# A hybrid decoder layer on one core: two factor broadcasts placed later among the first projections, and the last row statistics placed half a gate earlier

## The chip, the core and the metric

The kernel runs on one core of a Trainium2 chip. A core has a matrix engine (TensorE, PE in the profile), a vector engine (VectorE, DVE), an activation engine (ScalarE, ACT), GpSimd (POOL) and a queue engine that issues transfers (SyncE, SP). The metric is the device time of one execution in microseconds (us). Before the change it is 1122.99 us (median of 3 runs, 1122.89 to 1123.69). A difference of about 0.2%, some 2.2 us, is what a measurement of this kernel can tell from none.

## What is computed

One decoder layer on 512 tokens of width 1024, all in float32. A retention branch and a latent attention branch read the same normalised input through one combined projection; their gated sum goes through an output projection into the residual; then a squared-ReLU MLP, then a gated per-layer embedding. The parts that the change touches are these:

```python
h = rms_norm(x, norm_mix)
proj = h @ w_in
rq, rk, rv, rg, cq, ckv, krope, gr, gm = split(proj)
cq, ckv = rms_norm(cq, q_lat_norm), rms_norm(ckv, kv_lat_norm)
q = cq @ w_uq                       # 8 heads of 128 + 64
kv = ckv @ w_ukv                    # 8 heads of 128 (keys) + 128 (values)
k = concat(k_nope, krope)           # the 64 rotary columns are shared by the heads
q, k = rms_norm(q, q_norm), rms_norm(k, k_norm)     # then rotated by position
mixed = sigmoid(gr) * a_ret + sigmoid(gm) * a_mla
...
gate = sigmoid(rms_norm(x, norm_ple) @ w_ple_gate)
return x + gate * (p_l @ w_ple)
```

## The kernel before

Tokens lie along the free axis (512 columns) and channels along the 128 partitions, so a projection is a row of 128x512 matmuls into one bank of PSUM. Every float32 operand is split into a high and a low half (`split`, L301: ScalarE writes the high half, VectorE the low half), and a product is three matmuls, low by high, high by low, high by high (`mm3`, L291). Weights come as chunks: a transfer into a raw buffer (`wr_`, L243, six buffers), a copy on ScalarE (`wh_`, L261) and a subtraction on VectorE (`wl_`, L265), three buffers each. A chunk's split is queued one chunk ahead of its use (`AHEAD`), its transfer three ahead (`PREP`).

The work is a list of steps written by hand (`step`, L207; the list is L1119 to L1310). `run_steps` records them in that order, and the matmuls stay in it. The order of the other engines' instructions is set by a scheduler when the program is built, from the order of recording and what each needs. A step with a key uses a chunk of weights; a step without one uses none. PSUM has eight banks in the first part, each held until its last reader is done.

Row normalisation is postponed: the input enters its projections with its gain but unnormalised (`xg`), and sums of squares give factors that are multiplied in later. `first_stats` (L431) turns the first sums around with four transposes (`fst`) and computes on VectorE, in small instructions of a few columns, first `rx` (the input's inverse root mean square, by three Newton rounds, `rsqrt`, L322), then `rl` (the same for the two latents, again three rounds), from them `rho`, and `f` (the buffers `f1` and `f2`, by which values and statistics are scaled). A factor holds one number for each token, on partitions; to multiply a tile that has tokens along its columns, it is broadcast by four transposes on TensorE (`bcast`, L342). Two such broadcasts are touched here: `x_factor` (L459) writes `prx` from `rx`, which ScalarE copies into `rbc`, and `rotary_key` (L507) writes `prho` from `rho`, after which VectorE rotates the shared key columns (`t`, `krot`) and the split gives `kph` and `kpl`, which the attention scores (`sc`) read.

Around them stand `kq_head` (keys and queries of one head, `pk` and `pq`), `value_pair` (values of two heads, `pv`, 24 matmuls of 256 columns, scaled by `f` on their way out), `query_rotary` (`pqa`, `pqb`, 18 matmuls), `rotary_out` (rotates the query columns on VectorE, `o` and `qt`, and sends sixteen copies `qp` by SP's queue), `gate_out` (L685, multiplies a finished gate `gm` by `rbc` into `zm`, which goes to memory), and `fill` (L1112), which takes the next half gate from a list of fillers: 12 matmuls of the gate `gm` that nothing nearby waits for. `rotary_stats` (`sqr`), `pair_sums` (`sums`), `pair_stats` (`st`, then `ha`, `hr`) and `head_factor` (`pbk`) lead on to the first scores.

At the end, `turn` transposes the MLP's result back and adds the residual, `token_stats` (L955) sums squares into `stx` and computes `rx3`, `token_factor` (L962) broadcasts that into the same PSUM tile and ScalarE copies it out as `bcx`. `ple_gate` (L1088) computes gate `n` (`pg`, 24 matmuls, in two halves of 12 where `part` is given), and `ple_out` (L1097) multiplies it by `bcx`, takes the sigmoid (`zg`), multiplies by `pw`, adds and stores. This part has four PSUM tiles of two banks each.

Of the kernel before, what the change touches and what calls it, by code (L numbers as in the profile page):

```python
# [147 lines left out]
def trunk_layer(ctx: ExitStack, tc: tile.TileContext, xT, pT, pos, gains, const, decay, wstream, outT):  # L148
# [58 lines left out]
    def step(key, fn, *args):  # L207
        steps.append((key, fn, args))
# [903 lines left out]
    def fill(n=1):  # L1112
        for _ in range(n):
            if fillers and fillers[0][0] is None:
                step(*fillers.pop(0))
            if fillers:
                step(*fillers.pop(0))
# [11 lines left out]
    step(("kq", 0), kq_head, 0)  # L1129
    step(None, first_stats)  # L1130
    step(("kq", 1), kq_head, 1)
    step(None, x_factor)
    step(None, gate_out, 0)
    step(None, rotary_key)
    step(("v", 0), value_pair, 0)
    step(("qr", 0), query_rotary, 0)
    step(None, mask_parts)
    step(None, rotary_out, 0)
    fill(3)
    step(None, rotary_stats, 0)  # L1140
    step(None, pair_sums, 0)
    fill(1)
# [153 lines left out]
    step(("ple", 1), ple, 3)  # L1296
    step(None, turn, 2)
    step(None, turn, 3)
    for part in range(2):
        for n in range(2):  # L1300
            step(("pg", n), ple_gate, n, part)
    step(None, token_stats, "x3", "sq3")
    step(("pg", 2), ple_gate, 2)
    step(None, token_factor, "x3")
    step(None, ple_out, 0)
    step(None, ple_out, 1)
    step(None, ple_out, 2)
# [47 lines left out]
```

## Time and profile before

| what | number |
|---|---|
| time, median of 3 runs | 1122.99 us |
| the profiled execution's own time | 1123.06 us |
| its span, first to last instruction | 1121.3 us |
| TensorE busy | 1102.3 us |
| VectorE, ScalarE, GpSimd busy | 735.2, 537.2, 85.6 us |
| mean transfer rate over the span | 157 GB/s |

The span leaves out 1.76 us of the execution's own time. A row of the waits says which engine and line waited, for whom, the total in us, how often, and the longest. A row of the timeline has the start, the duration, engine, line, operation, tiles and shapes; in square brackets stands the idle time ahead of it and what ended it. A matmul's duration is longer than its distance to the next, since neighbours overlap; distances are taken from starts.

### The profile page before, as it was taken

What the parts mean: (1) busy time and instruction counts of PE and PEld (TensorE: products, weight loads), DVE (VectorE), ACT (ScalarE), POOL (GpSimd) and SP (SyncE); (2) the same over time, 40 slices, a digit from 0 to 9 for tenths busy, and PEclk for the clock granted to TensorE, in tenths of its full rate; (3) what the DMA queues carried; (4) which work ended last, traced back from release to release, by engine and by line L of the source; (5) the groups of instructions that cost most, each with busy time, mean ns of one, the idle gap of its engine ahead of it and who ended that gap; (6) DMA issues with size and microseconds to landing.
All of it is one profiled execution on the core that took longest, in us unless ns stands there. A gap on an engine that the chain in (4) does not pass through costs nothing.

```text
span 1121.3 us, 14666 instructions
## 1 busy us (share of the span) xinstructions
PE 1102.3 (98%) x5529; PEld 933.9 (83%) x5529; DVE 735.2 (66%) x1195; ACT 537.2 (48%) x763; POOL 85.6 (8%) x113
## 2 busy tenths in 40 slices
PE   9979999999999999999999999999999999999998
PEld 6767888888889889888988987888888888888877
DVE  7677676656776845855683677555465666668675
ACT  7635656453365435355544544434443444445542
POOL 0000000000110020021003000010100100101000
PEclk9989999999999999999999999999999999999999
DMA  7224131356787274589639754693755755738401
GB/s 256 70 70 133 53 104 61 126 180 216 197 220 185 98 201 130 151 176 256 161 105 216 218 179 158 190 283 107 179 160 163 184 164 153 184 122 227 139 29 76
DMA packets 59223, 175.97 MB, mean 157 GB/s; under 512 B 7248, under 2 KB 8656, under 8 KB 58896
## 3 DMA queue, kind: packets, MB, share of 16 engines
q1 hardware_dynamic: 45168, 129.66, 34.1%
q0 software_dynamic: 13840, 45.36, 20.9%
q8 instruction: 43, 0.70, 0.2%
q14 instruction: 28, 0.23, 0.1%
q10 hardware_dynamic: 144, 0.03, 0.0%
HBM read 156.92 MB, written 15.99 MB: 154 GB/s over the span
## 4 chain that ended last, share of the span: by engine, by line
PE 92%; DVE 3%; ACT 2%; issue 1%; DMA 1%; SPq 0%; DVEq 0%; ACTq 0%
PE up L168 16%; PE dn L168 14%; PE rg L168 7%; PE rv L168 7%; PE br L168 6%; PE pg L168 4%; PE gr L168 4%; PE rq L168 4%; PE bm L168 4%; PE rk L168 4%; PE gm L168 4%; PE wo L168 4%; PE ro L168 3%; PE sc L168 2%; PE pcq L168 1%; PE rs L168 1%
## 5 line engine op out<-in xcount | busy, mean ns | idle before, releaser
L168 PE MATMUL dn<-wh_dn,cl 128*128 128x512 f32 x224 | 87.2, 389 | 0.0
L168 PE MATMUL dn<-wh_dn,ch 128*128 128x512 f32 x224 | 87.2, 389 | 0.0
L168 PE MATMUL dn<-wl_dn,ch 128*128 128x512 f32 x224 | 87.1, 389 | 0.0
L261 ACT ACTIVATE wh_dn<-wr_dn 128x1024 fp32r<-128x1024 f32 x32 | 34.0, 1062 | 75.5 <-PE up L168 54.3
L261 ACT ACTIVATE wh_up<-wr_up 128x1024 fp32r<-128x1024 f32 x32 | 34.0, 1061 | 58.0 <-PE up L168 29.3
L265 DVE TENSOR_TENSOR wl_dn<-wr_dn,wh_dn 128x1024 fp32r<-128x1024 f32 x32 | 39.1, 1220 | 27.5 <-ACT wh_dn L261 27.5
L265 DVE TENSOR_TENSOR wl_up<-wr_up,wh_up 128x1024 fp32r<-128x1024 f32 x32 | 39.1, 1222 | 18.2 <-ACT wh_up L261 18.1
L265 DVE TENSOR_TENSOR wl_rg<-wr_rg,wh_rg 128x1024 fp32r<-128x1024 f32 x20 | 24.5, 1224 | 38.7 <-ACT wh_rg L261 38.3
L168 PEld LDWEIGHTS dn<-wh_dn,cl 128*128 128x128 f32 x224 | 42.1, 188 | 8.8
L168 PEld LDWEIGHTS dn<-wh_dn,ch 128*128 128x128 f32 x224 | 42.1, 188 | 8.8
L980 DVE SCALAR_TENSOR_TENSOR f<-up,bcx 128x512 f32<-128x512 f32 x32 | 20.6, 686 | 43.8 <-PE up L168 43.8
L168 PEld LDWEIGHTS dn<-wl_dn,ch 128*128 128x128 f32 x224 | 42.1, 188 | 8.6
L261 ACT ACTIVATE wh_dn<-dr_dn 128x1024 fp32r<-128x1024 f32 x24 | 25.5, 1060 | 41.6 <-PE up L168 28.8
L223 POOL DMA_DIRECT2D dr_dn<-wstream x24 | 21.7, 906 | 305.4 <-DMA dr_dn<-wstream 181.9
L265 DVE TENSOR_TENSOR wl_dn<-dr_dn,wh_dn 128x1024 fp32r<-128x1024 f32 x24 | 29.3, 1222 | 22.1 <-ACT wh_dn L261 22.1
L261 ACT ACTIVATE wh_rv<-wr_rv 128x1024 fp32r<-128x1024 f32 x28 | 29.7, 1060 | 28.1 <-PE rv L168 11.5
L261 ACT ACTIVATE wh_rg<-wr_rg 128x1024 fp32r<-128x1024 f32 x28 | 29.5, 1055 | 25.8 <-DMA wr_rg<-wstream 20.5
L265 DVE TENSOR_TENSOR wl_br<-wr_br,wh_br 128x1024 fp32r<-128x1024 f32 x16 | 19.5, 1221 | 21.6 <-ACT wh_br L261 21.6
L1038 DVE TENSOR_TENSOR d<-d,dn 128x1024 f32<-128x1024 f32 x24 | 29.3, 1219 | 6.5 <-PE dn L168 6.5
L265 DVE TENSOR_TENSOR wl_rv<-wr_rv,wh_rv 128x1024 fp32r<-128x1024 f32 x20 | 24.4, 1224 | 12.2 <-ACT wh_rv L261 12.2
L869 ACT ACTIVATE rt<-br 128x512 f32<-128x512 f32 x24 | 14.3, 597 | 36.1 <-PE br L168 30.7
L223 POOL DMA_DIRECT2D wr_rg<-wstream x16 | 13.9, 870 | 161.2 <-DVE wl_br L265 93.1
(1813 smaller groups left out, 3620.5 us busy)
## 6 DMA issues: line engine op xcount, KB each, us to landing
wr_up<-wstream SPq DMA_DIRECT2D x32, 512.0 KB, 4.4
wr_dn<-wstream SPq DMA_DIRECT2D x32, 512.0 KB, 3.5
dr_dn<-wstream POOLq DMA_DIRECT2D x24, 512.0 KB, 7.4
wr_rv<-wstream SPq DMA_DIRECT2D x20, 512.0 KB, 4.1
wr_rg<-wstream SPq DMA_DIRECT2D x20, 512.0 KB, 4.5
wr_rv<-wstream POOLq DMA_DIRECT2D x16, 512.0 KB, 6.0
wr_rg<-wstream POOLq DMA_DIRECT2D x16, 512.0 KB, 7.5
wr_br<-wstream SPq DMA_DIRECT2D x16, 512.0 KB, 3.5
```

The source lines that it names most:

```text
L168: return tc.keep_in_program_order(nc.tensor.matmul(*a, **k))
L223: nc.gpsimd.dma_start(raw, chunk(("w", blk, kb, fb, c)), accum_op=ALU.add)
L261: i = ACT(hi, raw, AF.Copy, scale=sign)
L265: TT(lo, raw, hi.bitcast(F32), op=ALU.subtract)
L869: ACT(t, ps, AF.Copy)
L980: STT(u[:, i], ps[:, i], 0.0, V["bcx2"], op0=ALU.max, op1=ALU.mult)
L1038: TT(to, to, dps[p], op=ALU.add if sign > 0 else ALU.subtract)
```

## The change

Two places of the step list are reordered; no instruction is added or taken away.

```diff
     step(("kq", 1), kq_head, 1)
+    step(("v", 0), value_pair, 0)
     step(None, x_factor)
     step(None, gate_out, 0)
-    step(None, rotary_key)
-    step(("v", 0), value_pair, 0)
     step(("qr", 0), query_rotary, 0)
     step(None, mask_parts)
     step(None, rotary_out, 0)
-    fill(3)
+    fill(1)
+    step(None, rotary_key)
+    fill(2)
     step(None, rotary_stats, 0)
...
     step(None, turn, 3)
-    for part in range(2):
-        for n in range(2):
-            step(("pg", n), ple_gate, n, part)
+    for n in range(2):
+        step(("pg", n), ple_gate, n, 0)
+    step(("pg", 0), ple_gate, 0, 1)
     step(None, token_stats, "x3", "sq3")
-    step(("pg", 2), ple_gate, 2)
+    step(("pg", 1), ple_gate, 1, 1)
+    step(("pg", 2), ple_gate, 2, 0)
     step(None, token_factor, "x3")
+    step(("pg", 2), ple_gate, 2, 1)
     step(None, ple_out, 0)
```

In the first place the values of the first pair go ahead of the broadcast of `rx`, and the broadcast of `rho` with the rotation of the key goes behind the rotary queries and one half gate. Keyed steps keep their order, so chunks are fetched in the same order as before.

TensorE's order after the second head's queries `pq`, before the change (each row is one matmul, output<-inputs and its shape, x4 four alike):

```order
L168 MATMUL pq_602<-cq2l,wh_kq_494 128x512
L168 MATMUL pq_602<-cq2h,wh_kq_494 128x512
L168 MATMUL prx<-cst,rx 128x128 x4
L168 MATMUL prho<-cst,rho 128x128 x4
L168 MATMUL pv_652<-wh_v_585,ckv0l 128x256
L168 MATMUL pv_652<-wl_v_586,ckv0h 128x256
```

The same place of TensorE's order after the change, with the middles of the groups `pv`, `pqa`, `pqb` and `gm` left out:

```order
L168 MATMUL pq_602<-cq2h,wh_kq_494 128x512
L168 MATMUL pv_624<-wh_v_585,ckv0l 128x256
...
L168 MATMUL pv_643<-wh_v_585,ckv1h 128x256
L168 MATMUL prx<-cst,rx 128x128 x4
L168 MATMUL pqa_679<-cq0h,wl_qr_621 128x512
...
L168 MATMUL gm_750<-xg3h,wh_gm_0_675 128x512
L168 MATMUL prho<-cst,rho 128x128 x4
L168 MATMUL gm_750<-xg4h,wl_gm_1_747 128x512
```

24 matmuls of `pv` now stand ahead of `prx`, and these with 18 of `pqa` and `pqb` and 12 of `gm` ahead of `prho`. Behind that half gate comes its second half, and then the next gate's first half (`gm_808`), which reads the weight half `wl_gm_0_783`.

On VectorE, in the difference where `rl` is computed, rows with a minus stood there before and rows with a plus stand there now (`al` is what `rl` is the inverse root of, `nt` a scratch tile, `ad` and `skr` parts of the key's statistics):

```order
-L687 TENSOR_TENSOR zm_625<-gm_454,rbc 128x512
+L577 COPY ad_826<-skr 128x4 x2
 L325 TENSOR_SCALAR rl<-al 128x8
-L510 TENSOR_TENSOR t_634<-kz,tmc 64x512
+L577 COPY ad_830<-skr 128x4 x2
 L326 TENSOR_SCALAR rl<-rl 128x8
-L511 SCALAR_TENSOR_TENSOR t_635<-kz,cst,tms 64x512
+L577 COPY ad_1721<-skr 128x4 x2
 L328 TENSOR_TENSOR nt_556<-rl 128x8
```

The wide `zm` and the two wide products `t`, and a third `t` a few rows below, have left the chain of `rl`; one wide `wl_gm_1_747` has come into it.

VectorE's order behind the first low halves of the values, after the change, down to the weight half that the second gate needs:

```order
L687 TENSOR_TENSOR zm_669<-gm_454,rbc 128x512
L312 SCALAR_TENSOR_TENSOR v00l<-pv_624,f_570,v00h 128x256
L312 SCALAR_TENSOR_TENSOR v01l<-pv_643,f_570,v01h 128x256
L555 SCALAR_TENSOR_TENSOR o_705<-pqa_679,gn,tmc 128x512
L556 SCALAR_TENSOR_TENSOR qt_708<-pqa_679,gn,tms 128x512
L557 SCALAR_TENSOR_TENSOR qt_707<-pqb_689,gn,tms 128x512
L558 SCALAR_TENSOR_TENSOR o_706<-pqb_689,gn,tmc 128x512
L559 TENSOR_TENSOR o_705<-o_705,qt_707 128x512
L560 TENSOR_TENSOR o_706<-o_706,qt_708 128x512
L561 TENSOR_TENSOR sa_701<-sa_701,sb_702 128x512
L307 TENSOR_TENSOR qr10l<-o_705,qr10h 128x512
L265 TENSOR_TENSOR wl_gm_0_783<-wr_gm_0_780,wh_gm_0_782 128x512
```

The rotation of the key, which stood ahead of the values' low halves, has moved behind this piece, between and behind the weight halves of the following gates; `zm` has moved into it.

At the end, TensorE's order after the change around the sums of squares `stx` (the first gates are `pg_9442` and `pg_9461`, the third `pg_9524`, the fourth `pg_9579`):

```order
L168 MATMUL pg_9442<-x3g7h,wh_pg_9357 128x512
L168 MATMUL stx_9486<-ones,sq_9434 128x1 x4
L168 MATMUL pg_9461<-x3g4h,wl_pg_9437 128x512
...
L168 MATMUL pg_9524<-x3g3h,wh_pg_9455 128x512
L168 MATMUL stx_9486<-cst,rx_9492 128x128 x4
L168 MATMUL pg_9524<-x3g4h,wl_pg_9456 128x512
...
L168 MATMUL pg_9579<-x3g0h,wl_pg_9519 128x512
```

Before, the sums stood behind the last matmul of `pg_9461`, 12 matmuls later, and the broadcast behind the last of the third gate, straight ahead of the fourth. The distance between the two stays at 24 matmuls.

## The prediction

> **What bounds the kernel now.** I read the page first, then TensorE's waits, then the granted clock by stretch, then the timelines around the longest waits. The page's first two parts and its chain:
>
> ```profile
> span 1121.3 us, 14666 instructions
> PE 1102.3 (98%) x5529; PEld 933.9 (83%) x5529; DVE 735.2 (66%) x1195; ACT 537.2 (48%) x763; POOL 85.6 (8%) x113
> PE 92%; DVE 3%; ACT 2%; issue 1%; DMA 1%; SPq 0%; DVEq 0%; ACTq 0%
> ```
>
> TensorE is the bound, busy for 98% of the span and 92% of the chain. A reordering can gain only where TensorE stands still or runs slowly: some 19 us in all. Its waits, longest first:
>
> ```profile
> PE prho L168 <- DVE rl L451: 6.1, 1, 6.1
> PE pg L168 <- ACT bcx L965: 1.2, 1, 1.2
> PE prx L168 <- DVE rx L330: 1.1, 1, 1.1
> PE pbk L168 <- DVE hr L603: 1.0, 1, 1.0
> ```
>
> The first three are the waits at the moved steps. The windows view (length, busy time and instructions of the five engines, granted clock, DMA) shows a second loss behind them:
>
> ```profile
> 54.50:62.50 8.00, 0.82 (x6) 0.46 (x5) 7.53 (x42) 2.98 (x7) 0.72 (x1) 0.79 0.30 104
> 63.20:67.40 4.20, 4.20 (x27) 4.20 (x26) 2.54 (x4) 1.33 (x3) 0.00 (x0) 0.67 0.00 0
> 112.40:115.40 3.00, 3.00 (x28) 2.93 (x25) 0.82 (x4) 2.76 (x8) 0.00 (x0) 1.00 0.00 0
> 1089.00:1095.00 6.00, 6.00 (x26) 4.96 (x27) 4.40 (x7) 1.38 (x3) 0.00 (x0) 1.00 0.21 83
> ```
>
> In the first window TensorE is busy for 0.82 of 8 us, while VectorE works for 7.53: it computes the factors. In the second, the values of the first pair run at a granted clock of 0.67 and take 4.2 us; the same 24 matmuls of the next pair take 3.0 at 1.00 (third window). So an idle of 6.1 us drops the clock. One of 1.2 us does not: the fourth window, behind the wait for `bcx`, shows 1.00.
>
> **The change, step by step.** The places on TensorE's timeline, in the order of before:
>
> ```profile
> 54.27 0.39 PE L168 MATMUL pq<-cq2h,wh_kq 128*128 128x512 f32 x1
> 55.77 0.65 PE L168 MATMUL prx<-cst,rx 128*128 128x128 f32 x4 [1.12 <-DVE rx L330]
> 62.48 1.09 PE L168 MATMUL prho<-cst,rho 128*128 128x128 f32 x4 [6.06 <-DVE rl L451]
> 77.03 0.50 PE L168 MATMUL gm<-xg0h,wl_gm 128*128 128x512 f32 x1
> 40.70 5.44 PE gm L168 x24
> 84.80 0.44 PE st L168 x4
> ```
>
> The two last rows are of the chain: 24 matmuls of 512 columns take 5.44 us, 0.227 each; four transposes with the restart behind them 0.44. The row at 77.03 is the first matmul of the second gate `gm`, from where TensorE's order is as before. The question of the first place is when that matmul starts.
>
> TensorE alone: `pv` follows `pq` at 54.27 + 0.23 = 54.5 and takes 3.0 at full clock, to 57.5. `prx` finds `rx` done (55.7) and takes 0.44. The 18 matmuls of the rotary queries take 4.1, to 62.0, the half gate 12 x 0.227 = 2.7, to 64.7, `prho` 0.44, the second half 2.7: **67.9**. By TensorE alone the gain is 77.0 - 67.9 = 9.1: the waits of 7.2, the slow clock's 1.2 in `pv`, and 0.7 of slow or delayed broadcasts.
>
> VectorE holds the weight half `wl_gm` of that matmul, behind the values and the whole rotation of the queries. Its rows before:
>
> ```profile
> 57.53 0.69 DVE L687 TENSOR_TENSOR zm<-gm,rbc 128x512 f32<-128x512 f32 x1
> 58.21 0.68 DVE L510 TENSOR_TENSOR t<-kz,tmc 64x512 f32<-64x512 f32 x1
> 59.00 0.75 DVE L511 SCALAR_TENSOR_TENSOR t<-kz,cst,tms 64x512 f32<-64x512 f32 x1
> 59.93 0.68 DVE L512 TENSOR_TENSOR t<-t,t 64x512 f32<-64x512 f32 x1
> 62.45 0.17 DVE L454 TENSOR_SCALAR f<-rl 128x4 f32<-128x4 f32 x1
> 67.68 0.48 DVE L312 SCALAR_TENSOR_TENSOR v00l<-pv,f,v00h 128x256 fp32r<-128x256 f32 x1 [0.54 <-ACT v00h L309]
> 68.09 0.48 DVE L312 SCALAR_TENSOR_TENSOR v01l<-pv,f,v01h 128x256 fp32r<-128x256 f32 x1
> 70.32 0.75 DVE L555 SCALAR_TENSOR_TENSOR o<-pqa,gn,tmc 128x512 f32<-128x512 f32 x1 [0.62 <-ACT sa L552]
> 70.98 0.74 DVE L556 SCALAR_TENSOR_TENSOR qt<-pqa,gn,tms 128x512 f32<-128x512 f32 x1
> 73.75 0.68 DVE L559 TENSOR_TENSOR o<-o,qt 128x512 f32<-128x512 f32 x1
> 74.34 0.69 DVE L560 TENSOR_TENSOR o<-o,qt 128x512 f32<-128x512 f32 x1
> ```
>
> By the distances of starts a wide two-input instruction costs 0.60, a three-input one 0.66, one of 256 columns 0.4. Four wide ones leave the chain of `rl` (3 x 0.60 + 0.66 = 2.5) and one `wl_gm` enters (0.6). The removed ones also filled gaps in which the chain waited for itself; I leave 0.2 for that. So `f` comes 1.7 sooner, at 60.8. ScalarE's first value copy and its hand-over take some 0.8 (an estimate: one half of this size, 0.48 in the rows of VectorE, and the two hand-overs), so the first `v00l` starts at 61.6. From there to the end of `wl_gm` stand four value halves (1.6), `zm` (0.6), four three-input products (2.6), three sums (1.8), `qr10l` (0.6) and `wl_gm` itself (0.7): 7.9 us, to 69.5. The rotary key, which goes behind this, isn't in it. The second gate starts at **69.6**, and a wait of 1.7 is new. Gain of the first place: 77.0 - 69.6 = **7.4 us**. The bounds of the new wait, which no row shows: nothing, if ScalarE and VectorE overlap better (gain 9.1), and twice as much (gain 5.7); I take the middle, which is the sum of the rows.
>
> Does it last? The rotary key's three products, two `krot` and `kpl`, 3.7 us on VectorE, ran while TensorE stood still or in `pv`. They now go between 69.6 and the first head's statistics, where VectorE waited before:
>
> ```profile
> 80.89 0.24 DVE L578 TENSOR_TENSOR ad<-sqr,f 128x8 f32<-128x8 f32 x2 [1.52 <-PE sqr L168]
> 84.84 0.69 DVE L687 TENSOR_TENSOR zm<-gm,rbc 128x512 f32<-128x512 f32 x1 [3.11 <-PE gm L168]
> 89.07 0.17 DVE L603 TENSOR_TENSOR hr<-hr,f 128x16 f32<-128x16 f32 x1
> 90.57 1.03 PE L168 MATMUL pbk<-cst,hr 128*128 128x128 f32 x8
> 90.77 0.69 DVE L687 TENSOR_TENSOR zm<-gm,rbc 128x512 f32<-128x512 f32 x1 [0.70 <-PE gm L168]
> 75.68 1.23 SPq L567 DMA_DIRECT2D qp<-qr10h  x2
> 85.70 0.58 SPq L567 DMA_DIRECT2D qp<-qr20l  x1
> ```
>
> 1.52 + 3.11 of idle time take 3.7 with 0.9 to spare. `hr` is done 1.3 us ahead of its broadcast; the new order puts a weight half of 640 columns in front of its last steps (0.75, by the 0.60 of 512), and 0.6 remains. The sixteen copies `qp` on SP's queue move with `qr10h`, some 7 us sooner, and the first scores, which need four of them, come behind `pbk`, 15 us after the first issue. Without that cover each microsecond of lateness is one of TensorE's. From 90.77 to 109 the chain runs over VectorE and ScalarE (the angles, the exponentials), but its start waits 0.70 for TensorE's gate, so it moves along. Here I count nothing. `gate_out` keeps the first gate's bank 4 to 5 us longer; the eight banks just suffice, since values and `zm` are read before 69.6. SP's and POOL's queues keep their orders.
>
> The last place:
>
> ```profile
> 1077.35 0.68 DVE L1084 TENSOR_TENSOR sq<-sq 128x512 f32<-128x512 f32 x1
> 1078.06 0.40 PE L168 MATMUL pg<-x3g4h,wl_pg 128*128 128x512 f32 x1
> 1084.98 0.16 DVE L330 SCALAR_TENSOR_TENSOR rx<-nt,rx 128x4 f32<-128x4 f32 x1
> 1087.19 0.60 PE L168 MATMUL stx<-cst,rx 128*128 128x128 f32 x4
> 1088.98 0.50 PE L168 MATMUL pg<-x3g0h,wl_pg 128*128 128x512 f32 x1 [1.19 <-ACT bcx L965]
> ```
>
> The fourth gate starts 1.79 behind the broadcast, because it takes over the PSUM tile that ScalarE is still copying out; without the wait it would be 0.44, so 1.35 are to be had. The broadcast now ends half a gate, 2.7 us, ahead of the fourth gate, which covers that. The sums of squares move to 1078.06, and `sq` is done at 1078.03: a tie, for which I take off 0.05. `rx3` keeps its slack of 2 us before the broadcast. Gain: **1.3 us**, bounds 0.9 (`sq` late by half a microsecond) and 1.4.
>
> **Sum:** 7.4 + 1.3 = 8.7. The profiled execution took 1123.06, so **1114.36**; the median lies 0.07 below it: **1114.3 us**.
>
> [...] The clock was kept at an idle of 1.2 us and lost at one of 6.1; the new wait of 1.7 is near the first, so the sum has no slow clock in it. [...] The rows here leave open where between 1.2 and 6.1 it falls.
>
> **The rivals.**
> 1. *VectorE's backlog returns part of it.* If the 3.7 us of the key don't fit, `pbk` waits. At worst all but the slack of 1.3 shows: 2.4, so 1116.7. Against it: the idle time sums to 4.6.
> 2. *The clock falls at the new wait*: 1.2 more, 1115.5. Against it: the fourth window.
> 3. *The first gain is hidden anyway.* If the VectorE and ScalarE chain from 90 to 109 did not move with TensorE, the scores would come when they came before, and only the end would gain: 1121.7. Against it: that chain's start waits for TensorE.
> 4. *Slower: the query copies come late.* The sixteen copies stand on SP's queue behind two weight loads that wait for buffers. If these held the copies, the first scores would wait for `qp`. They are needed just behind `pbk`, at about 84; each microsecond beyond that is one of the total, so from a landing at 84 + 8.7 = 92.7 the kernel is slower than before, and with copies at 95 it takes 1125. Against it: the buffers are freed sooner than before, and even the last copy, issued at 85.7 before, would be issued at 78.7, 14 us ahead of that point.
>
> **How the numbers follow.** Forecast 0.76; rival 1 0.09, rival 2 0.07, rival 3 0.05, rival 4 0.03. The forecast and the first two rivals are faster by more than 0.2% (2.2 us, about what a measurement can tell from no change): 0.92. Rival 3 is within it, 0.05; rival 4 slower, 0.03. The range goes down to 1112.3 (no new wait: 1.7, and some more) and up to 1117.0, which takes in the doubled wait with an end that gains 0.9 (1116.5) and the first two rivals.
>
> **What would show it.** In TensorE's waits the rows of `prho`, `prx` and `pg` on `bcx` are gone, and one of `gm` on `wl_gm`, 1.7, is new. `pv` shows a clock of 1.00 and 3.0 us. The second gate starts at 69.6, `pbk` near 83.2, the fourth gate of the end 8.7 sooner with no wait. I am wrong if `pbk` or the scores show a new wait, if the clock drops behind 68, or if the first matmul of the second gate starts behind 71.

## The result and the profile after

| kernel | median (runs) | ratio to before, 95% interval |
|---|---|---|
| before | 1122.94 us (1122.50 to 1123.69, 4 runs) | 1 |
| changed | 1114.07 us (1113.85 to 1117.37, 4 runs) | 0.9929 [0.9912, 0.9946] |

The change takes off 8.87 us; 8.7 were forecast. One of the four runs took 1117.37, the other three lie within 0.4 of each other.

The page of the changed kernel, its span, its engines and the chain that ended last:

```profile
span 1112.4 us, 14663 instructions
PE 1100.3 (99%) x5529; PEld 932.8 (84%) x5529; DVE 734.8 (66%) x1195; ACT 536.9 (48%) x763; POOL 85.8 (8%) x113
PE 92%; DVE 4%; ACT 1%; DMA 1%; issue 1%; SPq 0%; DVEq 0%; ACTq 0%
```

The span is 8.9 shorter, but TensorE's busy time only 2.0: most of what went was standing still, and the 2.0 are mostly matmuls that had run at a slow clock (1.3 of them in `pv`, 4.2 us before and 2.87 now). Its waits, the longest but for one of 1.5 at the start that both kernels have:

```profile
PE gm L168 <- DVE wl_gm L265: 1.5, 1, 1.5
...
PE pbk L168 <- DVE hr L603: 1.0, 1, 1.0
PE sc L168 <- ACT sqk L526: 0.8, 1, 0.8
PE pt0a L168 <- DVE p L652: 0.7, 1, 0.7
```

The rows of `prho` (6.1), `prx` (1.1) and `pg` on `bcx` (1.2) are gone, and one of `gm` on `wl_gm` is new. The row of `pbk` is no news: it belongs to a later pair of heads (at 161 us, before at 169) and stood there before with the same 1.0. The windows view of the first place, first over the window that held TensorE's long idle before, then over the values, then over the new wait (columns as in the prediction, granted clock third from the end):

```profile
54.50:62.50 8.00, 8.00 (x49) 7.05 (x48) 7.46 (x47) 4.71 (x12) 0.00 (x0) 1.00 0.30 93
53.80:56.80 3.00, 3.00 (x27) 2.96 (x26) 2.79 (x15) 2.60 (x6) 0.00 (x0) 1.00 0.29 87
67.40:70.00 2.60, 1.05 (x6) 0.90 (x6) 2.60 (x5) 1.15 (x2) 0.00 (x0) 1.00 0.25 64
```

VectorE works as hard in the first window as before (7.46 to 7.53), but TensorE is now busy for all of its 8 us instead of 0.82. The clock stays at 1.00, also through the new wait. TensorE's timeline at the points that the prediction named:

```profile
53.67 0.39 PE L168 MATMUL pq<-cq2h,wh_kq 128*128 128x512 f32 x1
53.89 0.28 PE L168 MATMUL pv<-wh_v,ckv0l 128*128 128x256 f32 x1
56.76 0.60 PE L168 MATMUL prx<-cst,rx 128*128 128x128 f32 x4
64.06 0.60 PE L168 MATMUL prho<-cst,rho 128*128 128x128 f32 x4
68.95 0.47 PE L168 MATMUL gm<-xg0h,wl_gm 128*128 128x512 f32 x1 [1.54 <-DVE wl_gm L265]
```

From the last `pq` to the second gate it is 68.95 - 53.67 = 15.28 us; before it was 77.03 - 54.27 = 22.76. The place gained **7.48**. Distances must be taken here: executions reach this stage up to 0.8 us apart (the marks `fst` in the table below), which lies ahead of the change. VectorE's rows on the path of that wait:

```profile
59.98 0.17 DVE L454 TENSOR_SCALAR f<-rl 128x4 f32<-128x4 f32 x1
60.84 0.48 DVE L312 SCALAR_TENSOR_TENSOR v00l<-pv,f,v00h 128x256 fp32r<-128x256 f32 x1 [0.19 <-ACT v00h L309]
68.12 0.69 DVE L265 TENSOR_TENSOR wl_gm<-wr_gm,wh_gm 128x512 fp32r<-128x512 f32 x1
81.97 0.17 DVE L603 TENSOR_TENSOR hr<-hr,f 128x16 f32<-128x16 f32 x1
```

From the start of `v00l` to the end of `wl_gm` VectorE works 7.97 us without a gap, and TensorE waits for that end. `hr` ends at 82.14. The end of the kernel:

```profile
1060.42 1.91 PE L168 MATMUL tr<-cst,d 128*128 128x128 f32 x16
1069.86 0.68 DVE L1084 TENSOR_TENSOR sq<-sq 128x512 f32<-128x512 f32 x1
1070.68 1.02 PE L168 MATMUL stx<-ones,sq 128*128 128x1 f32 x8
1077.77 0.60 ACT L965 ACTIVATE bcx<-stx 128x512 f32<-128x512 f32 x1 [2.09 <-PE stx L168]
1080.33 0.39 PE L168 MATMUL pg<-x3g0h,wl_pg 128*128 128x512 f32 x1
```

`sq` ends at 1070.54, just ahead of its sums at 1070.68; `bcx` is copied 2 us ahead of the fourth gate, which starts with no wait.

### The profile page after: what moved, and what is told of

Same layout as the page of the kernel before. It is cut to its first block, busy times and chain, and to the rows that moved or that the text cites. A ratio compares the mean times of both kernels' runs of the same rounds, so it can differ in the third digit from the quotient of the medians.

```text
span 1112.4 us, 14663 instructions
## 1 busy us (share of the span) xinstructions
PE 1100.3 (99%) x5529; PEld 932.8 (84%) x5529; DVE 734.8 (66%) x1195; ACT 536.9 (48%) x763; POOL 85.8 (8%) x113
## 4 chain that ended last, share of the span: by engine, by line
PE 92%; DVE 4%; ACT 1%; DMA 1%; issue 1%; SPq 0%; DVEq 0%; ACTq 0%
PE up L168 16%; PE dn L168 14%; PE rg L168 7%; PE rv L168 7%; PE br L168 6%; PE pg L168 4%; PE gr L168 4%; PE rq L168 4%; PE bm L168 4%; PE rk L168 4%; PE wo L168 4%; PE gm L168 3%; PE ro L168 3%; PE sc L168 2%; PE pcq L168 1%; PE rs L168 1%
```

## The experiments

All times were taken beside the kernel before on the same chip. The changed kernel itself ran beside experiments 4 to 6; 1, 2, 3 and 7 ran on another chip. To see the first place by itself I also take, from each trace, the distance from the transposes of the first statistics (`fst`, which stand ahead of both moved steps) to the first head's broadcast `pbk` (which stands behind everything that was moved there):

| kernel | median us (runs) | ratio to before | `fst` | `pbk` | distance |
|---|---|---|---|---|---|
| before | 1122.94 (the 4 above) | 1 | 50.61 | 90.57 | 39.96 |
| changed, beside the runs | 1113.93 (1113.85 to 1114.66) | 0.9920 [0.9907, 0.9932] | 50.12 | 82.58 | 32.46 |
| first place alone | 1115.06 (1114.80 to 1115.61) | 0.9929 [0.9917, 0.9942] | 50.12 | 82.53 | 32.41 |
| last place alone | 1121.26 (1120.60 to 1122.44) | 0.9985 [0.9976, 0.9994] | 49.92 | 90.78 | 40.86 |
| key back, values moved | 1119.16 (1117.56 to 1120.16) | 0.9963 [0.9950, 0.9975] | 49.86 | 87.80 | 37.94 |
| values back, key moved | 1114.24 (1113.79 to 1115.72) | 0.9920 [0.9906, 0.9933] | 50.32 | 83.21 | 32.89 |
| key's products doubled | 1117.59 (1115.45 to 1119.60) | 0.9947 [0.9934, 0.9961] | 50.68 | 85.19 | 34.51 |
| queries' rotation later | 1119.73 (1118.66 to 1120.27) | 0.9968 [0.9957, 0.9980] | 50.09 | 88.55 | 38.46 |
| sums into the new wait | 1112.54 (1112.14 to 1112.85) | 0.9906 [0.9893, 0.9920] | 50.20 | 81.58 | 31.38 |

**1. The first place alone.** The end's part of the diff undone.

> The first place alone; the end as before. Theory (the two places gain apart from each other, 7.4 to 7.5 us in the first and 1.2 to 1.3 in the last): 1115.4 us, the second gate's first matmul at 69.0 with a wait of 1.5 on wl_gm, and the wait of pg on bcx back at 1.2. Rival (the places are not independent: part of the first gain only reaches the end because the end was loosened too, for instance through weights that are fetched earlier): behind 1116.5.

Measured: 1115.06, the wait on `wl_gm` 1.5, and that of `pg` on `bcx` back at 1.2. The distance of the first place is the whole change's to 0.05. The rival (and with it the prediction's third, that the first gain is hidden behind the chain of VectorE and ScalarE) falls.

**2. The last place alone.** The first place's part undone.

> The last place alone; the first as before, with its waits of 6.1 at prho and 1.1 at prx. Theory: 1121.7 us, gain 1.2 to 1.3, no wait of pg on bcx, and nothing new ahead of the sums of squares or of the broadcast. Rival (the copy of bcx only trades its wait for one of the sums of squares, which come half a gate sooner and tie with sq): 0.5 or less, 1122.4 or more.

Measured: 1121.26. The gain of 1.7 has an interval of 0.7 to 2.7; the rows are finer. From the last `tr` to the fourth gate:

```profile
1068.23 1.91 PE L168 MATMUL tr<-cst,d 128*128 128x128 f32 x16
1088.12 0.39 PE L168 MATMUL pg<-x3g0h,wl_pg 128*128 128x512 f32 x1
```

That is 19.89. In the kernel before the last `tr` is this row, and its fourth gate starts at 1088.98:

```profile
1067.91 1.91 PE L168 MATMUL tr<-cst,d 128*128 128x128 f32 x16
```

So it was 21.07, and 1.18 are gained up to the gate; up to the end of the span (1120.3 and 1121.3) 1.32. No wait of the sums shows; they start 0.36 behind the matmul ahead of them, 0.23 before, so their coming sooner cost about 0.1, and the rival falls. In the first place this execution stood 0.9 us worse than the kernel before, with the same order: its clock was slow for longer there (10.3 us against 6.9), which is taken up below.

**3. Only the values moved.** The key's broadcast goes back:

```diff
     step(("v", 0), value_pair, 0)
     step(None, x_factor)
     step(None, gate_out, 0)
+    step(None, rotary_key)
     step(("qr", 0), query_rotary, 0)
     step(None, mask_parts)
     step(None, rotary_out, 0)
-    fill(1)
-    step(None, rotary_key)
-    fill(2)
+    fill(3)
```

> Both places, but the rotary key goes back directly behind the gate's multiplication; only the values stay ahead of the two broadcasts. Theory (TensorE, ahead of time here, waits for what VectorE has yet to compute; the key's products then stand in the chain of rl again): a wait of 2.5 to 3 at prho, one of about 1 at sqr, none on wl_gm, 2.4 us above the whole change: 1116.5. If a wait of 3 us drops the granted clock, 1.2 more: 1117.7. Rival (the values' move alone fills the wait, and where the key stands is of no account): 1114.1. Rival (the key's move alone carries the gain): 1120 or more.

Measured: 1119.16, higher than either expectation. The waits are as expected (2.65 at `prho`, 1.10 at `sqr`), but the clock fell twice, behind the wait of 2.65 and behind the one of 1.10:

```profile
57.20:59.90 2.70, 0.06 (x2) 0.07 (x2) 2.46 (x19) 0.29 (x1) 0.00 (x0) 1.00 0.61 153
60.00:64.00 4.00, 4.00 (x14) 3.17 (x14) 3.79 (x14) 2.06 (x5) 0.72 (x1) 0.57 0.18 74
64.00:67.00 3.00, 3.00 (x15) 2.46 (x14) 1.09 (x3) 0.63 (x1) 0.00 (x0) 1.00 0.16 64
74.00:75.50 1.50, 0.40 (x3) 0.03 (x1) 1.50 (x4) 1.20 (x3) 0.00 (x0) 1.00 0.00 0
77.00:81.00 4.00, 4.00 (x17) 2.80 (x10) 2.21 (x5) 0.60 (x1) 0.57 (x1) 0.57 0.56 165
81.00:83.00 2.00, 2.00 (x12) 1.68 (x11) 0.91 (x3) 0.74 (x1) 0.00 (x0) 1.00 0.33 85
```

A mean of 0.57 over 4 us is 4 x 0.43 / 0.5 = 3.4 us at half the clock, both times, and TensorE was busy throughout: each costs some 1.7 (an estimate, half of 3.4; in the first, matmuls of 512 columns start 0.43 apart, and 0.23 apart behind it, which makes 1.6). 2.4 for the order and 2 x 1.7 make 5.8; the distance to `pbk` grew by 5.48. The profiled execution is one of three at 1119.2 to 1120.2 and a mean clock of 0.997; the two others took 1117.6 at 0.998, which fits one stretch in place of two, but they have no traces. The values' move alone does not fill the wait, so the rival of 1114.1 falls. Nor does the key's move alone carry all of the gain: against the kernel before, the values' move alone still took 2.0 off the distance, slow stretches included.

**4. Only the key moved.** The values go back behind the gate:

```diff
-    step(("v", 0), value_pair, 0)
     step(None, x_factor)
     step(None, gate_out, 0)
+    step(("v", 0), value_pair, 0)
     step(("qr", 0), query_rotary, 0)
```

> The rotary key's broadcast stays behind the queries and one half gate, but the values go back behind the broadcast of rx and the gate's multiplication. Theory (VectorE's queue sets the second gate, so what TensorE waits for at prx it would otherwise wait for at wl_gm): the wait of 1.1 at prx is back, the wait on wl_gm falls to 0.5, zm stands in the chain of rl again and costs some 0.5: 1114.6 us. Rival (the waits add up: what the values' move removed comes back whole): 1.1 or more, 1115.2 and up. Two waits of at most 1.1 us should leave the clock at 1.00.

Measured: 1114.24, with runs that overlap those of the whole change (1113.93). Its waits:

```profile
PE prx L168 <- DVE rx L330: 1.1, 1, 1.1
...
PE gm L168 <- DVE wl_gm L265: 0.7, 1, 0.7
```

The wait of 1.1 at `prx` is back, and 0.9 of it has been taken out of the one on `wl_gm`. The distance to `pbk` is 0.43 longer, no more than the wide `zm` that stands in the chain of `rl` again. So the key's move by itself gains nearly all of the first place, 7.1 of 7.5 by the distances; added to it, the values' move is worth about 0.4 by the rows, and nothing that the times can tell. The 7.1 and the 2.0 of run 3 do not add up to 7.5, since both moves fill the same waits.

**5. The key's products doubled.** Its first two products and the two `krot` are recorded twice:

```diff
-        TT(t1[0:64], kz[0:64], V["cm"][0:64], op=ALU.mult)
-        STT(t2[0:64], kz[64:128], cst[64:128, C_SGN:C_SGN + 1], V["sn"][64:128], op0=ALU.mult, op1=ALU.mult)
+        for _ in range(2):
+            TT(t1[0:64], kz[0:64], V["cm"][0:64], op=ALU.mult)
+            STT(t2[0:64], kz[64:128], cst[64:128, C_SGN:C_SGN + 1], V["sn"][64:128], op0=ALU.mult, op1=ALU.mult)
         TT(t1[0:64], t1[0:64], t2[0:64], op=ALU.add)
-        TT(kr[0:64], t1[0:64], prh[0:64], op=ALU.mult)
-        TT(kr[64:128], t1[0:64], prh[0:64], op=ALU.mult)
+        for _ in range(2):
+            TT(kr[0:64], t1[0:64], prh[0:64], op=ALU.mult)
+            TT(kr[64:128], t1[0:64], prh[0:64], op=ALU.mult)
```

> The whole change, with the key's first two products and its two krot products each recorded twice (four more VectorE instructions of 512 columns, 2.9 us by the distances of starts); the values are the same. Theory (the key's 3.7 us fit into 4.6 us of VectorE's idle time with 0.9 to spare): 2.0 us above the whole change, 1116.1, and a wait that is new ahead of the first scores, at pbk or earlier. Rival (VectorE has idle time enough in this stage, as its share of 66% would have it): no change, 1114.1. Rival (the stage is bound by VectorE throughout): all of it, 1117.

Measured: `pbk` 34.51 behind `fst`, 2.05 more than the changed kernel, the amount of the first theory: of 2.9 us of added work 0.85 would have found room. The time is 1117.59 in the median, but its runs spread over 4 us. TensorE's waits:

```profile
PE st L168 <- ACT sums L590: 1.9, 1, 1.9
PE gm L168 <- DVE wl_gm L265: 1.5, 1, 1.5
```

The new wait isn't at `pbk`: it is at `st`, for the copy `sums` on ScalarE. The last `krot` on VectorE, and ScalarE's queue behind it:

```profile
76.44 0.68 DVE L516 TENSOR_TENSOR krot<-t,prho 64x512 f32<-64x512 f32 x1
77.44 0.74 ACT L261 ACTIVATE wh_kq<-wr_kq 128x640 fp32r<-128x640 f32 x1 [4.09 <-PE gm L168]
78.08 0.61 ACT L306 ACTIVATE kph<-krot 128x512 fp32r<-128x512 f32 x1
78.60 0.58 ACT L590 ACTIVATE sums<-sums 128x512 f32<-128x512 f32 x1
```

Two things delay the copy. `krot` ends late, at 77.12, and `kph` and `sums` stand behind it. And the scheduler has put the weight half `wh_kq` ahead of both in this program, where the changed kernel has it behind them (`kph` at 74.26, `sums` at 74.80, `wh_kq` at 76.77); it started only as TensorE's gate ended. In the changed kernel `kph` starts 0.03 behind the end of `krot`, here 0.96 behind. Without that 0.93 the delay would be some 1.1 us (an estimate, which no run sets apart). So about half of the 2.05 comes from VectorE's added work, and that the amount met the theory is in part chance.

Of the 3.7 us by which this execution's span is longer than the changed kernel's beside it (1115.8 and 1112.1), 2.05 lie in the place, 0.6 ahead of `fst` and 1.1 behind `pbk`. In that last stretch, some 240 us later, the retention part's matmuls `rv` wait for 0.9 in all; such waits are 1.0 in run 4, 0.3, none and 0.2 in three executions of the changed kernel, and none in the others. Two of the five runs had a mean clock of 0.998, which fits a slow stretch, but they have no traces: how much of the spread is owed to this edit stays open.

**6. The queries' rotation behind the key.**

```diff
-    step(None, rotary_out, 0)
     fill(1)
     step(None, rotary_key)
-    fill(2)
+    fill(1)
+    step(None, rotary_out, 0)
+    fill(1)
```

> Another order: the rotation of the queries is recorded behind the rotary key, between the second and the third half gate, so that the weight halves go ahead of it on VectorE. Theory: the wait on wl_gm is gone, the statistics of the queries' rotary part (sqr) come later on VectorE and TensorE waits for sa some 4.5 us in one piece: 3.0 above the whole change, 1117.1, if the clock holds; 1118.8 to 1120.5 if the wait drops it for one window or two. Rival (only the wait on wl_gm binds): 1112.6.

Measured: 1119.73. The wait on `wl_gm` is gone, and one of 4.4 at `sqr` for `sa` has come, so the rival falls. The clock behind it, again by windows:

```profile
70.20:74.60 4.40, 0.02 (x1) 0.00 (x0) 4.40 (x8) 1.82 (x3) 0.57 (x1) 1.00 0.28 113
75.00:81.80 6.80, 6.80 (x24) 4.38 (x24) 1.63 (x5) 0.60 (x1) 0.00 (x0) 0.50 0.39 98
81.90:84.00 2.10, 2.10 (x13) 1.71 (x12) 1.13 (x3) 0.74 (x1) 0.19 (x1) 1.00 0.38 95
```

6.8 us at half the clock, twice the 3.4 of run 3 and so the expectation's two: 3.0 of order and 3.4 of clock make 6.4, and the distance grew by 6.0.

**7. The first pair's sums and the key's broadcast inside the new wait.** Four matmuls of ones, which stood behind the queries' statistics, go ahead of the second gate. They stand between the halves of the first gate and push what follows into the wait; the broadcast of `rho` stood ahead of the second gate already, half a gate sooner:

```diff
     fill(1)
+    step(None, pair_sums, 0)
+    fill(1)
     step(None, rotary_key)
-    fill(2)
+    fill(1)
     step(None, rotary_stats, 0)
-    step(None, pair_sums, 0)
     fill(1)
     step(None, pair_stats, 0)
```

> The whole change, and the sums of the first pair of heads (pair_sums, four matmuls of ones) and the broadcast of rho are put ahead of the second gate's first matmul, into the new wait on wl_gm; nothing is taken away. Theory (VectorE's queue fixes when wl_gm is ready, so TensorE's other work fits into the wait at no cost): the wait falls from 1.5 to 0.5, the total to 1113.1. Rival (the head's factors hr have only 0.3 us of slack, so a second gate that ends sooner only turns the wait on wl_gm into one at pbk): 0.3 us or less, 1113.8.

Measured: 1112.54. TensorE's rows in the new place:

```profile
68.19 0.60 PE L168 MATMUL prho<-cst,rho 128*128 128x128 f32 x4
69.05 0.50 PE L168 MATMUL gm<-xg0h,wl_gm 128*128 128x512 f32 x1 [0.26 <-DVE wl_gm L265]
```

The second gate starts when it did (18.85 us behind `fst` against 18.94), the wait falls from 1.54 to 0.26, and `pbk` comes 1.08 sooner: what TensorE does ahead of that matmul is free up to the wait's length. The rival falls: `hr` moved along, since the sums it is computed from came sooner. This is the fastest order of all. It was run once more, with the changed kernel beside it.

> The order of the earlier run with the first pair's sums and the broadcast of rho inside the new wait, again, now beside the changed kernel on one chip. If its 1.4 us below the changed kernel are its own: 1112.3 to 1112.9 in every run at a mean clock of 1.000, none of the runs overlapping with the other kernel's. If 0.4 of it was the run-to-run spread in the middle of the kernel and only the removed wait of 1.0 to 1.3 counts: 1112.9 to 1113.1.

> The changed kernel once more, beside the others on one chip, to see how often its new wait of 1.5 us costs the clock. If 1.5 us never drop it: all runs within 0.5 of 1114.0 at a mean clock of 1.000 or 0.999. [...]

> The changed kernel a third time, as the measure for the run beside it: 1113.9 to 1114.1 median. A run near 1117.4, like one of the first four, would come at a mean clock of 0.998; if none comes in ten further runs, it is rare.

Measured: the new order 1112.76 (1112.59 to 1113.32), ratio 0.9910 [0.9895, 0.9926]; the changed kernel beside it 1114.14 (1113.52 to 1115.19), ratio 0.9923 [0.9910, 0.9935]. The runs do not overlap, though one of the four lies above the 1112.9 that was expected, and the distance is again 1.4, of which the rows of the place explain 1.1. The other 0.3 stays open. The changed kernel's ten further runs lie between 1113.52 and 1115.19 at mean clocks of 0.999 and 1.000; none was like the 1117.37, which had 0.998. That clock fits one slow stretch, but a stretch costs 1.7, half of the 3.3 by which the run was longer; no trace of it exists, and the rest stays open.

## Why the prediction was right

- **TensorE alone ready at 67.9, the second gate at 69.6.** Both held, as distances from `pq`: 13.6 forecast and 67.41 - 53.67 = 13.74 measured; 15.3 and 15.28. That the absolute time was 68.95 is the execution's earlier start.
- **VectorE sets the second gate.** Forecast: `f` 6.5 behind `pq`, `v00l` 7.3, then 7.9 to the end of `wl_gm`. Measured: 6.31, 7.17, 7.97. Run 7 shows the mechanism: other work of TensorE's ahead of the gate cost it nothing.
- **The slow clock is saved.** `pv` ran 2.87 us at 1.00, against 4.2 at a mean of 0.67 before.
- **The end.** Forecast 1.3, measured 1.2 up to the fourth gate and 1.3 to 1.4 up to the end of the span. The tie of `sq` was one: it ended 0.14 us ahead of its sums, which start 0.35 behind the matmul ahead of them instead of 0.23, so the 0.05 taken off for it was a little too small.
- **Rival 1, the backlog.** VectorE's waits between 68 and 90 us in the changed kernel:

```profile
DVE ad L578 <- PE sqr L168: 0.7, 1, 0.7
DVE zm L687 <- PE gm L168: 0.3, 1, 0.3
DVE wl_kq L265 <- DMA qp<-qr20l: 0.3, 1, 0.3
```

  1.52 and 3.11 of idle time have become 0.7 and 0.3: the key's work went there, with little left. Run 5 does not confirm the forecast of 0.9 to spare, though 0.85 found room there: about half of its delay came from the place of `wh_kq`, and without that some 1.8 of the 2.9 would have found room (the estimate above). The place of the rival was wrong too: the prediction watched `pbk` behind `hr`, and the wait comes at `st`, through ScalarE's queue, which the prediction did not follow there.
- **Rival 2, the clock.** That a wait of 1.7 would leave the clock alone was the author's estimate from the 1.2 at `bcx`. A wait of 1.5 did not cost it, in the changed kernel's profiled executions (1.53 to 1.56, the clock at 1.00 behind it) and in that of run 1 (1.54, the matmuls behind it 0.23 apart). But the price of the rival, 1.2, was too low: a slow stretch costs some 1.7 where TensorE has work for all of it (the estimate of run 3), and runs 3 and 6 lost two. And the upper end of the range took the new wait at twice its size without a price for the clock. Run 3 had slow stretches behind a wait of 2.65, less than the doubled 3.4; with one such stretch that end would be 1116.5 + 1.7 = 1118.2, above the stated 1117.0. The range held because the wait was as forecast, not because its end was well founded.
- **Rival 3** fell with runs 1 and 2; **rival 4** did not come: the first scores follow `pbk` with no wait, and the copies `qp` are issued from 67.1 on, instead of 75.68.
- **The credit for the values' move** was never split from the key's in the sum. The waits that it removes, 1.1 at `prx`, were counted in the 9.1 of TensorE alone, which VectorE cuts to 7.4; run 4 shows that this cut eats nearly all of the values' part. Nor does any run split the key's own gain, between the work that TensorE now has ahead of `prho` and the products that left the chain of `rl` (`f` comes 6.31 behind `pq` instead of 8.18).
- **The 19 us to be had** were span less busy time. They hold the waits alone; the slow clock's 1.2 lies in the busy time and comes on top.

## What to carry to other kernels

When a waiting engine's work is reordered, follow the engine that it waited for up to the next thing that it owes: here the second gate's time came from VectorE's queue, so the values' move was worth about 0.4 beside the key's, while four matmuls whose result was needed later gained 1.1 once they stood ahead of the wait that was left. Follow the other queues as well: in run 5 a weight half on ScalarE stood in the way. Ask of every wait that stays whether the clock could fall behind it, as it did in run 3 behind 2.65 and behind 1.10, and price a slow stretch into the upper end of a range. Compare executions by distances between marks around the change, since their starts and far-off waits differ by more than many changes are worth.

## What the runs showed of the hardware

In these traces the granted clock fell to 0.50 for stretches of 3.4 us (run 3, twice), 6.8 (run 6), 6.9 (the kernel before) and 10.3 (the last place alone), near one, two and three times 3.4, and the wait ahead of one could be much shorter, as the 1.10 of run 3. The windows of the last two, the kernel before first:

```profile
59.00:66.00 7.00, 3.52 (x17) 3.55 (x18) 5.63 (x33) 0.63 (x1) 0.26 (x1) 0.51 0.13 51
57.00:67.30 10.30, 5.49 (x26) 5.52 (x27) 8.05 (x39) 1.58 (x3) 0.72 (x1) 0.50 0.16 57
```

These are 7.00 x 0.49 / 0.5 = 6.9 and 10.3, with the same order and the same wait of 6.1; the longer one is why run 2's execution stood 0.9 worse in that place: its `pv` took 5.04 us from the first matmul to the start of `pqa`, the kernel before's 4.16. The mean clocks fit this: the fifteen runs of the kernel before that stood beside the first experiments have 0.995 (seven, median 1123.7) or 0.996 and 0.997 (eight, median 1122.6), and one more 3.4 us at half the clock is 3.4 x 0.5 / 1121 = 0.0015 of the mean.

The length of one wait alone did not tell whether a stretch followed. In the traced executions, behind waits of 1.54 and of 1.88 (at `st` in run 5) the clock stayed at 1.00; behind the one of 2.65 in run 3 it fell to 0.50, and 2 us after the end of the one of 1.10 there it fell to 0.50 again, while behind the 1.12 at `prx` in run 4 it stayed at 1.00. Behind the 1.10 stood `sqr` and `sums`, matmuls of 4 columns and on 32 columns of the array. With the last place alone the clock fell at 57.0, where the window above begins, when the wait of 6.1 had lasted for only 1.3, with `prx` and a wait of 1.1 ahead of it. What decided where a stretch began, no run set apart.
